# A decoder trunk on one core: GpSimd casts the first weights, x's row blocks are turned in another order, and the low parts of one feed-forward weight tile are taken earlier

## The chip, the cores and the metric

The kernel runs on one core of a Trainium2 chip. The core has five engines that run side by side, each through its own list of instructions in order: TensorE (PE, and PEld for its weight loads) multiplies matrices, VectorE (DVE) and ScalarE (ACT) work element by element and can read the matrix results in PSUM, GpSimd (POOL) works element by element on SBUF, and SyncE (SP) issues most DMAs. An engine waits for another only through semaphores. The metric is the device time in microseconds (us); it is the median of three runs. Before the change it is 1012.55 us (1012.4 to 1013.15).

## What is computed

One layer on 512 rows of width 1024, in float32: a norm, one wide projection, three token mixers, a gated sum, an output projection onto the residual, a second norm, a convolutional feed-forward, and a last norm.

```python
u = rmsnorm(x, ln1_g[i])
proj = u @ w_in[i]
q, k, v, pool_in, z, xbc, dt_raw, gate_pre = jnp.split(proj, split_idx, axis=-1)
...
merged = gates[:, :, 0] * y_a + gates[:, :, 1] * y_b + gates[:, :, 2] * y_c
x = x + merged @ w_o[i]
x = x + conv_ffn(rmsnorm(x, ln2_g[i]), ffn_w_up[i], ffn_conv_w[i], ffn_conv_b[i], ffn_w_down[i])
...
def conv_ffn(u, w_up, conv_w, conv_b, w_down):
    h = causal_dwconv(u @ w_up, conv_w, conv_b)
    a, v = h[..., :D_FF], h[..., D_FF:]
    return (jax.nn.silu(a) * v) @ w_down
```

## The kernel before

Every matrix product is made in three passes. Each operand is split into a high part (a cast to fp32r) and a low part (the value less its high part), and TensorE sums high x high, high x low and low x high (`mm3`, L239). So each weight tile (128 partitions x 2048 elements, mostly) needs, after its DMA, a cast for the high part `wh` (ACT, `cast`, L195) and a subtraction for the low part `wl` (DVE, `low`, L217) before its products can end.

The order of the work on each engine is the order in which the program is written; nothing is rearranged. `trunk` makes a list of jobs, one for each weight tile. In the main loop at the end of it each job, n, is first "prepared": the low part of tile n+1 is taken, the high part of tile n+2 is cast, and the DMA of tile n+3 is issued (`prepare`). Then the job's matmuls are written. A few jobs are marked `late` and call their `prepare` themselves, in two halves: the first `next()` takes the low part of n+1, the second casts n+2 and fetches n+3.

Two places concern the change.

**The start (L1840 to L2000).** The first weight tile comes in two halves of 128 columns (`load_w0`, each 128 x 8 x 128 elements, 512 KB), after the first two row blocks of x. x comes in four row blocks (tb = 0 to 3) of 128 rows, each in two DMAs (`xin`, columns 0 to 511 and 512 to 1023). `turned(tb)` has TensorE transpose the eight 128 x 128 pieces k of a row block into PSUM. Piece k goes to PSUM bank k % 4, where k and k + 4 lie side by side; row block 1 uses three other banks by k % 3. `split_x(tb, k)` then scales each piece by the norm's gain and splits it: ACT writes the high part `xh`, DVE the low part `xl`. Seven matmuls on ones (`warm_up(STILL, 0)`) follow the transposes of row block 1. After that come the products of the first tile with columns 0 to 255 of the rows, by halves j = 0, 1 and by pairs: HH (`h0` x `xh`), HL (`h0` x `xl`), LH (`l0` x `xh`). On TensorE the order is: HH and HL of j = 0, HH of j = 1, the transposes of row block 2, HL of j = 1, LH of j = 0, the transposes of row block 3, LH of j = 1. The high part `h0` of half 0 is cast by DVE (two casts of 128 x 512, L1952), that of half 1 by ACT (L1959); both low parts `l0` are subtracted by POOL (`low0`, L1886).

**The opening of the feed-forward (`up_jobs`, `opening`).** The first two tiles of the up projection start on row blocks 0 and 1 while row blocks 2 and 3 are still being normed. Each of the last two row blocks needs a chain: DVE adds the last product to the residual x (L1376), ACT sums squares (L443), DVE works out the scale (L475 to L478), DVE and ACT scale the two halves of the row block (L482, L483), TensorE transposes them (L457), ACT and DVE split them into `uh` and `ul` (L460, L461). The list `late` holds what is left of the two chains. In half 0 `opening` runs `next(late[1])`, which is the DVE and ACT part of row block 3, then the products of tile 0, then the turn of row block 2, then `next(rest[0])`, the low part of the second up tile. In half 1 it runs two of the three products of tile 1, the turn of row block 3, and the product with that low part.

Of the kernel before, what the change touches and what calls it, by code (L numbers as in the profile page):

```python
# [19 lines left out]
KD = D // P  # L20
# [62 lines left out]
def trunk(ctx: ExitStack, tc, out, x, rel_bias, ln1_g, w_in, b_gate, w_a, pool_w, pool_scale, w_b,  # L83
# [3 lines left out]
    act, dve, pool, pe, sp = nc.scalar, nc.vector, nc.gpsimd, nc.tensor, nc.sync  # L87
# [21 lines left out]
    def MM(name):  # L109
        return psum.tile([P, S], F32, name=name, tag="mm")  # L110

    def SM(name):
        return psum.tile([P, S], F32, name=name, tag="sm")
# [41 lines left out]
    def step():  # L155
        flush()
        if waiting:
            running.append(iter(waiting.pop(0)))
        now = [(it, 0) for it in running]
        for phase in (0, ROWS, WHOLE, REST):  # L160
            now = [(it, advance(it, phase) if at == phase else at) for it, at in now]
# [65 lines left out]
    def wsrc(w, k0, k1, c0, c1):  # L227
        return w[k0 * P:k1 * P, c0:c1].rearrange("(k p) c -> p k c", p=P)
# [14 lines left out]
    def chunk_a(ps, ws, j, xh, xl, ks, lo=0, hi=S, k0=0):  # L243
        wh, wl = ws
        mm3(ps[:, lo:hi], lambda k: wh[:, k0 + k, j * P:(j + 1) * P],
            lambda k: wl[:, k0 + k, j * P:(j + 1) * P],
            lambda k: xh(k)[:, lo:hi], lambda k: xl(k)[:, lo:hi], ks)
# [1204 lines left out]
    def up_evac(m, ps):  # L1452
        t = HC[m] = T("hc")
        act.activation(t, ps, AF.Identity, bias=ff["c1"][:, ff["b"] + m:ff["b"] + m + 1], scale=fw(2, m))  # L1454
        for k in range(2):
            sh = 2 - k
            dve.scalar_tensor_tensor(t[:, sh:], ps[:, :S - sh], fw(k, m), t[:, sh:], OP.mult, OP.add)  # L1457
        if m < KF:
            act.activation(t, t, AF.Silu)  # L1459
            return  # L1460
        a = HC[m - KF]
        pool.tensor_tensor(a, a, t, OP.mult)  # L1462

        def later():
            yield
            k = m - KF
            if k % 2:
                h, l = T("fh", F32R), T("fl", F32R)
                act.copy(h, a)
                it = sums_of(HC[k - 1], a, T("sah", F32R), T("sal", F32R),  # L1470
                             lambda j, h, l: FS.__setitem__((j, k // 2), (h, l)), k >= KS)
                next(it)
                dve.tensor_sub(l, a, h.bitcast(F32))
                ACTS[k] = (h, l)
                yield
                for _ in it:
                    yield
                return
            t = T("f0", F32R)
            act.copy(t[:, :256], a[:, :256])  # L1480
            dve.tensor_sub(t[:, 256:], a[:, :256], t[:, :256].bitcast(F32))
            FS[0, k // 2] = (t[:, :256], t[:, 256:])

        running.append(later())
# [61 lines left out]
    def up_jobs():  # L1546
        held, rest = [], []

        def opening(job, half):
            def body(ws):  # L1550
                uh2, ul2 = nxt["uh"], nxt["ul"]
                if half == 0:
                    rest.append(job.prepare(later=True))
                    next(late[1])
                pss = [MM("pu") for _ in range(2)]

                def product(a, b, i):
                    for j in range(2):
                        for k in range(KD):
                            pe.matmul(pss[j][:, :256], a[:, k, j * P:(j + 1) * P], b[:, k, :256],  # L1560
                                      start=i + k == 0, stop=i == 2 and k == KD - 1)

                product(ws[0], uh2, 0)
                product(ws[0], ul2, 1)
                if half == 0:
                    product(ws[1], uh2, 2)
                next(late.pop(0), None)

                next(rest[0], None)
                if half:  # L1570
                    product(ws[1], uh2, 2)
                for j in range(2):
                    held.append((ws, j, pss[j], KF * half + j))
                if half == 0:
                    return
                for n, (ws_, j, ps, m) in enumerate(held):
                    chunk_a(ps, ws_, j, lambda k: uh2[:, k, :], lambda k: ul2[:, k, :], range(KD), 256, S)
                    if n == 1:
                        job.prepare()
                    up_evac(m, ps)  # L1580
                    step()
            return body

        for p in range(KF // 2):
            for half in range(2):
                def body(ws, p=p, half=half):
                    uh2, ul2 = nxt["uh"], nxt["ul"]
                    for j in range(2):
                        ps = MM("pu")
                        chunk_a(ps, ws, j, lambda k: uh2[:, k, :], lambda k: ul2[:, k, :], range(KD))  # L1590
                        up_evac(KF * half + 2 * p + j, ps)
                        step()
                c = half * DFF + p * 256
                job = Job([wsrc(w_up, 0, KD, c, c + 256)], KD, 256, body)
                if p == 0:
                    job.late = True
                    job.body = opening(job, half)
                yield job
# [258 lines left out]
    raw0 = w0.raw = wraw.tile([P, KD, 256], F32, name="raw", tag="raw")  # L1857
# [19 lines left out]
    h0 = w0.high = whp.tile([P, KD, 256], F32R, name="wh", tag="wh")  # L1877
# [3 lines left out]
    def part(j, k0, k1):  # L1881
        return slice(None), slice(k0, k1), slice(j * P, (j + 1) * P)

    def low0(j, k0, k1):
        o = part(j, k0, k1)
        pool.tensor_tensor(l0[o], raw0[o], h0[o].bitcast(F32), OP.subtract)  # L1886
# [6 lines left out]
    def block(tb, k):  # L1893
        if tb == 1:
            return (uT1, first[2], first[1])[k % 3][:, (k // 3 + 1) * P:(k // 3 + 2) * P]
        return bank(k)[:, tb % 2 * P:tb % 2 * P + P]

    def turned(tb):
        if tb % 2 == 0:
            banks[:] = [SM("uT") for _ in range(4)]  # L1900
        for k in range(KD):
            pe.transpose(block(tb, k), xin[tb, k // 4][:, (k % 4) * P:(k % 4 + 1) * P], eye)

    def split_x(tb, k):
        c = slice(tb * P, (tb + 1) * P)
        act.mul(xh[k][:, c], block(tb, k), g1[:, k:k + 1])
        dve.scalar_tensor_tensor(xl[k][:, c], block(tb, k), g1[:, k:k + 1],
                                 xh[k][:, c].bitcast(F32), OP.mult, OP.subtract)
# [33 lines left out]
    warm_up(WARM)  # L1942
    pe.transpose(first[2][:, :KD], g8[:KD, :P], eye[:KD, :KD])
    turned(0)
    dve.tensor_copy(g1, first[2][:, :KD])
    for k in range(KD):
        split_x(0, k)
    turned(1)
    for k in range(KD):
        if k == 2:  # L1950
            for k0 in (0, 4):
                dve.tensor_copy(h0[part(0, k0, k0 + 4)], raw0[part(0, k0, k0 + 4)])  # L1952
            low0(0, 0, KD)
        split_x(1, k)
    warm_up(STILL, 0)
    group(0, (HH,), 0, 256)
# [6 lines left out]
    half_squares(dve, 0, 1)  # L1963
    group(1, (HH,), 0, 256)
    turned(2)
    for k in range(KD):
        split_x(2, k)
# [112 lines left out]
```

## Time and profile before

| | |
|---|---|
| median of three runs | 1012.55 us (1012.4 to 1013.15) |
| the profiled execution | 1012.54 us, of which 1010.8 us from the first instruction to the last |
| PE busy | 999.7 us, 99% of the span |
| DVE, ACT, POOL busy | 753.7, 534.7, 137.8 us |
| DMA | 127.03 MB, 126 GB/s |

A row of the timeline reads: start, time from the first to the last of the merged instructions, engine, line, operation, output <- inputs, shapes, count, and in brackets the idle time of the engine before it with what ended that. All times are us from the start of the span. SPq and ACTq are DMAs being issued by SP and ACT; a DMA lands later.

### The profile page before, as it was taken

How to read it: one execution, taken by the hardware profiler on the slowest of the kernel's cores; microseconds unless marked ns; L12 is line 12 of the kernel's file. 1: busy time of each engine (PE TensorE's matmuls, PEld its weight loads, DVE VectorE, ACT ScalarE, POOL GpSimd, SP SyncE). 2: the span in 40 equal slices, each digit the busy share in tenths (PEclk: the TensorE clock that was granted, in tenths of full speed). 3: DMA queues.
4: the chain of work that ended last, by engine and by line, in shares of the span. 5: the costliest groups of instructions: out<-in, count | busy, mean ns of one | idle time of the engine just before them, and what ended most of it. 6: DMA issues, size and time to landing. Idle time of an engine off the chain costs nothing.

```text
span 1010.8 us, 13607 instructions
## 1 busy us (share of the span) xinstructions
PE 999.7 (99%) x5307; PEld 850.0 (84%) x5307; DVE 753.7 (75%) x962; ACT 534.7 (53%) x929; POOL 137.8 (14%) x111
## 2 busy tenths in 40 slices
PE   9999999999999999999999999999999999999996
PEld 8898878999988888888888888898888888888885
DVE  6995668677767645776889888868778768685877
ACT  6343546554445566888566246554444434443456
POOL 4400010110000000000044501302111100121032
PEclk9999999999999999999999999999999999999999
DMA  7344360755343435552254754232352134542573
GB/s 221 102 126 131 106 187 4 193 150 147 102 155 94 108 100 132 146 137 62 77 152 125 211 188 90 80 126 84 99 193 84 50 117 149 175 115 73 146 184 109
DMA packets 117735, 127.03 MB, mean 126 GB/s; under 512 B 6791, under 2 KB 96462, under 8 KB 117671
## 3 DMA queue, kind: packets, MB, share of 16 engines
q1 hardware_dynamic: 112327, 116.98, 37.4%
q0 software_dynamic: 5040, 8.65, 5.4%
q8 instruction: 42, 0.69, 0.3%
q10 hardware_dynamic: 304, 0.53, 0.1%
q14 instruction: 22, 0.18, 0.1%
HBM read 121.56 MB, written 3.00 MB: 123 GB/s over the span
## 4 chain that ended last, share of the span: by engine, by line
PE 96%; DVE 2%; ACT 0%; DMA 0%; issue 0%; ACTq 0%
PE pa L239 37%; PE pu L239 23%; PE pb L239 10%; PE pd L239 8%; PE pqk L239 6%; PE pq L239 3%; PE ps L810 1%; PE pa L1918 1%; PE ppw L239 1%; PE po L858 1%; PE pt L844 1%; PE py L1140 1%; DVE wl L217 1%; PE pyo L1147 1%; PE pst L1128 0%; DMA xin<-in_x_dram 0%
## 5 line engine op out<-in xcount | busy, mean ns | idle before, releaser
L217 DVE TENSOR_TENSOR wl<-raw,wh 128x2048 fp32r<-128x2048 f32 (+3 forms) x86 | 205.9, 2396 | 32.9 <-ACT wh L195 24.2
L195 ACT CAST wh<-raw 128x1024 fp32r<-128x1024 f32 (+2 forms) x168 | 167.0, 1011 | 53.0 <-DVE raw L362 17.8
L1457 DVE SCALAR_TENSOR_TENSOR hc<-pu,fcol,hc 128x510 f32<-128x510 f32 x88 | 65.9, 748 | 53.7 <-ACT hc L1454 52.0
L239 PE MATMUL pu<-uh,wh 128*128 128x512 f32 (+1 forms) x352 | 83.6, 379 | 0.0
L239 PE MATMUL pu<-uh,wl 128*128 128x512 f32 (+1 forms) x352 | 83.5, 379 | 0.0
L239 PE MATMUL pu<-ul,wh 128*128 128x512 f32 (+1 forms) x352 | 83.5, 379 | 0.0
L239 PE MATMUL pa<-uh,wh 128*128 128x512 f32 (+1 forms) x336 | 80.9, 380 | 0.0
L239 PE MATMUL pa<-ul,wh 128*128 128x512 f32 (+1 forms) x336 | 78.9, 374 | 0.0
L239 PE MATMUL pa<-uh,wl 128*128 128x512 f32 (+1 forms) x336 | 78.8, 374 | 0.0
L239 PEld LDWEIGHTS pu<-ul,wh 128*128 128x128 f32 x352 | 64.2, 188 | 12.5
L239 PEld LDWEIGHTS pu<-uh,wl 128*128 128x128 f32 x352 | 64.2, 188 | 12.4
L239 PEld LDWEIGHTS pu<-uh,wh 128*128 128x128 f32 x352 | 64.1, 188 | 12.4
L1454 ACT ACTIVATE hc<-pu,fcol,fcol 128x512 f32<-128x512 f32 x40 | 31.2, 779 | 75.7 <-PE pu L239 75.7
L239 PEld LDWEIGHTS pa<-ul,wh 128*128 128x128 f32 x336 | 60.7, 188 | 11.4
L239 PEld LDWEIGHTS pa<-uh,wl 128*128 128x128 f32 x336 | 60.7, 188 | 11.2
L239 PEld LDWEIGHTS pa<-uh,wh 128*128 128x128 f32 x336 | 59.4, 189 | 10.6
L1462 POOL TENSOR_TENSOR hc<-hc 128x512 f32<-128x512 f32 x22 | 29.9, 1360 | 279.0 <-DVE hc L1457 243.3
L217 DVE TENSOR_TENSOR wl<-w,wh 128x2048 fp32r<-128x2048 f32 (+1 forms) x26 | 54.3, 2088 | 9.8 <-issue 4.5
L195 ACT CAST wh<-w 128x1024 fp32r<-128x1024 f32 (+1 forms) x52 | 47.2, 950 | 8.6 <-DMA w<-in_ffn_w_down_dram 3.8
L832 ACT ACTIVATE sb<-sb,nmls 128x128 f32<-128x128 f32 (+1 forms) x72 | 30.0, 418 | 32.5 <-DVE nmls L829 21.9
L1459 ACT ACTIVATE hc<-hc 128x512 f32<-128x512 f32 x22 | 13.9, 633 | 40.3 <-DVE hc L1457 40.3
L1123 POOL TENSOR_TENSOR st<-st,dts 128x512 f32<-128x512 f32 x4 | 4.2, 1051 | 225.4 <-ACT st L1131 164.9
(461 smaller groups left out, 2012.8 us busy)
## 6 DMA issues: line engine op xcount, KB each, us to landing
raw<-in_w_in_dram SPq DMA_DIRECT2D x24, 1024.0 KB, 5.5
raw<-in_ffn_w_up_dram SPq DMA_DIRECT2D x22, 1024.0 KB, 5.1
raw<-in_w_in_dram SPq DMA_DIRECT2D x14, 512.0 KB, 4.0
raw<-in_w_in_dram SPq DMA_DIRECT2D x8, 768.0 KB
raw<-in_ffn_w_down_dram SPq DMA_DIRECT2D x6, 1024.0 KB, 4.9
raw<-in_w_b_dram SPq DMA_DIRECT2D x4, 1024.0 KB
al<-ad SPq DMA_DIRECT2D x16, 256.0 KB, 7.9
raw<-in_w_c_dram SPq DMA_DIRECT2D x4, 1024.0 KB, 5.3
```

Source lines behind the costliest of these rows:

```text
L195: (other.tensor_copy if other and i else act.copy)(job.high[:, :, o], job.raw[:, :, o])
L217: (eng or dve).tensor_tensor(l[:, :, o], job.raw[:, :, o], h[:, :, o].bitcast(F32), OP.subtract)
L239: pe.matmul(ps, l, r, start=first and n == 0, stop=last and n == total - 1, skip_group_check=onto)
L810: pe.matmul(pss[i][:, o:o + w * P], q[r, n * P:(n + 1) * P], k[r, kb * P:(kb + w) * P], start=True, stop=True)
L832: act.activation(sb[:, off:off + w * P], sb[:, off:off + w * P], AF.Exp, bias=nm[:, n, h:h + 1], accum_out=ls[:, n, h:h + 1])
L844: pe.transpose(pt[:, o:o + P], sb[:, o:o + P], eye)
L858: pe.matmul(po[DH * hh:DH * hh + DH, n * P:(n + 1) * P], V[g, kb + i][:, (2 * c + hh) * DH:(2 * c + hh + 1) * DH], probs[2 * c + hh, nb][: ...
L1140: pe.matmul(py[DH * i:DH * i + DH, j * P:(j + 1) * P], xc[:, o:o + DH], als[j // 2][:, lo:lo + P], start=True, stop=True)
L1454: act.activation(t, ps, AF.Identity, bias=ff["c1"][:, ff["b"] + m:ff["b"] + m + 1], scale=fw(2, m))
L1457: dve.scalar_tensor_tensor(t[:, sh:], ps[:, :S - sh], fw(k, m), t[:, sh:], OP.mult, OP.add)
L1459: act.activation(t, t, AF.Silu)
L1462: pool.tensor_tensor(a, a, t, OP.mult)
```

## The change

At the start, POOL instead of DVE casts half 0 of the first weight tile, ahead of POOL's own subtractions and with no DVE work in between; the casts no longer stand between DVE's splits of row block 1. The transposes of every row block are written in the order 0, 4, 1, 5, 2, 6, 3, 7, so that the two pieces of one bank follow each other; the splits keep the order 0 to 7. In the opening of the feed-forward, the low part of the second up tile is written ahead of row block 3's chain instead of behind row block 2's turn; the second half of that `prepare` (cast and fetch) stays in half 1.

```diff
@@ opening
                 if half == 0:
                     rest.append(job.prepare(later=True))
+                    next(rest[0])
                     next(late[1])
...
                 next(late.pop(0), None)
 
-                next(rest[0], None)
                 if half:
+                    next(rest[0], None)
                     product(ws[1], uh2, 2)
@@ turned
-        for k in range(KD):
+        for k in (0, 4, 1, 5, 2, 6, 3, 7):
             pe.transpose(block(tb, k), xin[tb, k // 4][:, (k % 4) * P:(k % 4 + 1) * P], eye)
@@ the start
     turned(1)
+    for k0 in (0, 4):
+        pool.tensor_copy(h0[part(0, k0, k0 + 4)], raw0[part(0, k0, k0 + 4)])
+    low0(0, 0, KD)
     for k in range(KD):
-        if k == 2:
-            for k0 in (0, 4):
-                dve.tensor_copy(h0[part(0, k0, k0 + 4)], raw0[part(0, k0, k0 + 4)])
-            low0(0, 0, KD)
         split_x(1, k)
```

On POOL, at the start of the program, this is the difference. The CAST rows are the casts of `h0`, the TENSOR_TENSOR rows of `wl` are the two subtractions. The row ISA is not written in the kernel: the build puts it there, and it is the instruction that has a library of GpSimd routines loaded. The build places one such instruction ahead of the first POOL instruction whose routine is in a library; a subtraction's is, a cast's is not.

```order
 L2062 MEMSET const-uint8-127 128x1
 L2076 UNCONDITIONAL_BRANCH
-L1886 ISA
-L1886 TENSOR_TENSOR wl<-raw,wh 128x8x128 x2
+L1951 CAST wh<-raw 128x4x128 x2
+L1887 ISA
+L1887 TENSOR_TENSOR wl<-raw,wh 128x8x128 x2
 L1973 TENSOR_TENSOR xf<-xh,xl 128x256 x8
 L642 TENSOR_TENSOR xf<-xf,rows 128x512 x8
```

Before, the ISA instruction was the first thing on POOL's list; now it stands behind two casts that need the weights from memory, and ahead of the first subtraction.

On DVE, in the opening of the feed-forward, these rows stood before. The `va`, `vo`, `v`, `r`, `rt`, `u` rows are row block 3's chain, the `ul` rows are the splits of row blocks 2 and 3, and the L217 row is the low part of the second up tile.

```order
L1376 TENSOR_TENSOR x_5515<-x_5515,pb 128x512
L1330 TENSOR_SCALAR va_106<-so_105 128x1
L1331 TENSOR_SCALAR vo_107<-va_106 128x1
L475 SCALAR_TENSOR_TENSOR v<-ss,vo_107 128x1
L476 RECIPROCAL r<-sq 128x1
L477 SCALAR_TENSOR_TENSOR rt<-r,v 128x1
L478 SCALAR_TENSOR_TENSOR rt<-rt,r 128x1
L482 SCALAR_TENSOR_TENSOR u_5961<-x_5515,rt,grow 128x512
L461 TENSOR_TENSOR ul_5789<-uT,uh_5788 128x4x128 x2
L217 TENSOR_TENSOR wl<-raw,wh 128x2048
L461 TENSOR_TENSOR ul_5789<-uT,uh_5788 128x4x128 x2
```

And these now, in the same place:

```order
L1376 TENSOR_TENSOR x_5515<-x_5515,pb 128x512
L1330 TENSOR_SCALAR va_106<-so_105 128x1
L1331 TENSOR_SCALAR vo_107<-va_106 128x1
L217 TENSOR_TENSOR wl<-raw,wh 128x2048
L475 SCALAR_TENSOR_TENSOR v<-ss,vo_107 128x1
L476 RECIPROCAL r<-sq 128x1
L477 SCALAR_TENSOR_TENSOR rt<-r,v 128x1
L478 SCALAR_TENSOR_TENSOR rt<-rt,r 128x1
L482 SCALAR_TENSOR_TENSOR u_5961<-x_5515,rt,grow 128x512
L461 TENSOR_TENSOR ul_5789<-uT,uh_5788 128x4x128 x4
```

The low part moved up by seven instructions, ahead of the scale of row block 3, and both row blocks' `ul` now follow each other.

## The prediction

> **What bounds the kernel now.** I read the page first, then the list of what TensorE waited for, then the timeline of the two places that the change touches.
>
> ```profile
> span 1010.8 us, 13607 instructions
> ...
> PE 999.7 (99%) x5307; PEld 850.0 (84%) x5307; DVE 753.7 (75%) x962; ACT 534.7 (53%) x929; POOL 137.8 (14%) x111
> ...
> PE 96%; DVE 2%; ACT 0%; DMA 0%; issue 0%; ACTq 0%
> ```
>
> ```profile
> PE pa L1854 <- DVE ones L1843: 1.1, 1, 1.1
> PE pa L1918 <- ACT xh L1906: 0.8, 1, 0.8
> PE pu L1560 <- DVE wl L217: 0.6, 1, 0.6
> PE uT L1902 <- DMA xin<-in_x_dram: 0.5, 1, 0.5
> ```
>
> TensorE is busy for 99% of the span, and the chain that ended last lies on it for 96%. The second fence is its whole list of waits: 3.0 us in four places. So nothing on the other engines can win more than a few us, but whatever makes TensorE wait anywhere is added in full, since nothing behind it has slack to give back. The change touches the second wait (the start) and the third (the opening of the feed-forward). The profiled execution took 1012.54 us, the median of the three runs is 1012.55 us, so sums against the one hold for the other.
>
> **The start, as it is.** These are rows of the timeline of the first 20 us.
>
> ```profile
> 1.06 3.85 PE L1854 MATMUL pa<-ones 128*128 128x128 f32 x20 [1.06 <-DVE ones L1843]
> ...
> 1.76 1.28 ACT L1847 ACT_TABLE_LOAD   x1 [1.76 <-issue]
> 2.60 1.06 SPq L1860 DMA_DIRECT2D raw<-in_w_in_dram  x2
> ...
> 5.61 1.20 PE L1902 MATMUL uT<-eye,xin 128*128 128x128 f32 x9 [0.55 <-DMA xin<-in_x_dram]
> 6.41 2.43 ACT L1906 ACTIVATE xh<-uT,g 128x128 fp32r<-128x128 f32 x9 [3.16 <-PE uT L1902]
> ...
> 7.41 1.73 PE L1854 MATMUL pa<-ones 128*128 128x128 f32 x14
> ...
> 9.41 0.76 DVE L1952 CAST wh<-raw 128x512 fp32r<-128x512 f32 x2
> ...
> 9.97 1.81 PE L1918 MATMUL pa<-xh,wh 128*128 128x256 f32 x8 [0.83 <-ACT xh L1906]
> ...
> 10.24 5.20 POOL L1886 TENSOR_TENSOR wl<-raw,wh 128x1024 fp32r<-128x1024 f32 x2 [9.80 <-DVE wh L1952]
> ...
> 10.46 0.37 ACT L1906 ACTIVATE xh<-pa,g 128x128 fp32r<-128x128 f32 x1 [0.56 <-DVE xl L1907]
> ...
> 11.62 1.10 PE L1918 MATMUL pa<-xl,wh 128*128 128x256 f32 x8
> ...
> 14.31 1.20 PE L1918 MATMUL pa<-xl,wh 128*128 128x256 f32 x8
> ...
> 15.34 1.12 PE L1918 MATMUL pa<-xh,wl 128*128 128x256 f32 x8
> ...
> 17.04 0.40 SPq L182 DMA_DIRECT2D raw<-in_w_in_dram  x1
> ...
> 17.41 1.20 PE L1918 MATMUL pa<-xh,wl 128*128 128x256 f32 x8
> ```
>
> The rows at 15.34 and 17.41 are the ones that decide: they are the LH products of halves 0 and 1, and they need POOL's two subtractions, which run from 10.24 to 15.44. Before, the first was done 2.7 us ahead of its product and the second 2.0 us ahead. The time from issue to landing of the two weight halves, and the costs of POOL's instructions by shape, are in these rows.
>
> ```profile
> raw<-in_w_in_dram SPq DMA_DIRECT2D x2, 512.0 KB, 6.0
> ```
>
> ```profile
> L908 POOL TENSOR_TENSOR o<-o,wb 128x512 f32<-128x512 f32 x9 | 16.3, 1840 | 8.1 <-DMA wb<-wd 8.1
> ...
> L1321 POOL TENSOR_TENSOR xg<-x,grow 128x512 f32<-128x512 f32 x4 | 9.2, 2299 | 16.7 <-DVE x L1376 16.7
> ...
> L1886 POOL TENSOR_TENSOR wl<-raw,wh 128x1024 fp32r<-128x1024 f32 x2 | 5.2, 2626 | 9.8 <-DVE wh L1952 9.8
> L1123 POOL TENSOR_TENSOR st<-st,dts 128x512 f32<-128x512 f32 x4 | 4.2, 1051 | 225.4 <-ACT st L1131 164.9
> ```
>
> **The casts on POOL.** Half 0 lands at about 2.60 + 6.0 = 8.6, so POOL can cast from 8.6 where DVE began at 9.41. No row shows a cast on POOL. From below, DVE does one in 0.42 (two in 0.76); from above, a POOL operation of the same 128x512 takes 2.30 with two inputs (L1321). The quick POOL row (1.05) has long idle time ahead of it, the slower ones come in crowded stretches, and from 8 to 12 us DVE is busy throughout:
>
> ```profile
> 2.00:4.00 2.00, 2.00 (x12) 2.00 (x11) 0.00 (x0) 1.25 (x2) 0.00 (x0) 1.00 0.80 170
> ...
> 8.00:9.00 1.00, 1.00 (x11) 0.95 (x9) 1.00 (x5) 1.00 (x6) 0.00 (x0) 1.00 1.21 292
> ...
> 11.00:12.00 1.00, 1.00 (x7) 0.85 (x8) 1.00 (x4) 1.00 (x4) 1.00 (x1) 1.00 1.05 384
> ```
>
> (columns: window, its length, busy time of PE, PEld, DVE, ACT, POOL, then granted clock, DMA share, GB/s). So I take 1.8 each, by L908, and the second ends at 8.6 + 3.6 = 12.2. By the Trainium skill, GPSIMD Engine Reference, section Elementwise, a good one-input loop over 512 elements takes 769 ns; two of them would be an estimated 1.5 us in place of 3.6 and the sum 2.1 us less. No run here shows which.
>
> **The library.** This is the step on which I rest the forecast. Before, the ISA instruction stood first on POOL's list, in 9.80 us in which POOL did nothing else (L1886). Whatever it costs was hidden there. Now POOL reaches it after the casts, at 12.2, with the subtractions queued right behind it and TensorE waiting for those. Its cost has no row. From below it is 0, since an idle engine shows nothing; from above 9.8, the idle time in which it had to be over. The nearest rows are a load of the same kind on another engine (ACT_TABLE_LOAD, 1.28) and a fetch from memory in this stretch (6.0 to landing, with the DMA engines full, share 1.05 to 1.21). Code has to be fetched and then taken in, so I add the two: 7.3. The Trainium skill, GPSIMD Engine Reference, section Instruction dispatch, speaks against the change: the first call to freshly loaded code pays about 6 us (5.95), with no instruction in the profile for it. By that figure the sum would be 1.3 us less; the idle time before agrees in that it would have hidden it.
>
> **What that does to TensorE.** The first subtraction starts at 8.6 + 3.6 + 7.3 = 19.5 and takes 2.4 (half of 5.20, less for the first), so LH of half 0 starts at 22.0 in place of 15.34: 6.7 later. The second subtraction ends at about 24.7; LH of half 1 would follow at 24.7 in place of 17.41, 7.3 later. Meanwhile TensorE has run out: with the second cast at 12.2 its HL starts at 12.7 in place of 11.62, so the HL product of half 1 (14.31, about 1.0 long) ends near 16.4, and it idles 5.6 us. After its idle time at the start it ran 20 records in 3.85 us, later 14 in 1.73, at which pace 20 take 2.5: 1.4 us lost to a slow array, though the granted clock of 2 to 4 us reads 1.00. The same after 5.6 us of idle puts LH of half 1 at 22.0 + 2.07 + 1.4 = 25.5, 8.1 later, which is past the 7.3. I take 8.0. The bounds: casts of 2.3 and a load of 9.8 give 8.6 + 4.6 + 9.8 + 2.4 = 25.4, hence 10.1 + 1.4 = 11.5; casts of 0.42 with no load leave the subtractions early.
>
> Late next are POOL's eight `xf` additions behind the subtractions and, on SP, the fetch of the third weight tile, which needs the raw buffer that the second subtraction reads. Before, that fetch was issued at 17.04 and its tile was wanted by TensorE at 35.4:
>
> ```profile
> 24.47 10.92 PE pa L239 x48
> 35.46 21.82 PE pa L239 x96
> ```
>
> Its 18 us shrink to about 43.4 - 24.7 = 18.7, so nothing more is lost.
>
> **DVE freed, and the order of the transposes.** ACT started its splits at 6.41, when the fifth transpose (the second of bank 0) was through; with pieces 0 and 4 first it can start after two, three steps of 0.11 earlier, 0.33. Without the two casts DVE saves 0.67 and ACT's 0.56 of waiting goes. So the first HL could come 1.0 earlier, and row blocks 2 and 3 might save 0.3. But the product behind them needs POOL's casts too, and those now end last, so here I count 0; these gains stand only in the rivals. A transpose of row block 1 asks for its second DMA 0.33 earlier; before it did not wait, and ACT needs that row block only 1 us later, so 0 too.
>
> **The opening of the feed-forward.**
>
> ```profile
> 660.13 0.15 DVE L1330 TENSOR_SCALAR va<-so 128x1 f32<-128x1 f32 x1
> ...
> 660.43 1.03 PE L457 MATMUL uT<-eye,u 128*128 128x128 f32 x8
> ...
> 661.22 2.15 PE L1560 MATMUL pu<-uh,wh 128*128 128x256 f32 x16
> ...
> 661.98 0.75 DVE L482 SCALAR_TENSOR_TENSOR u<-x,rt,grow 128x512 f32<-128x512 f32 x1
> 662.03 0.72 ACT L483 ACTIVATE u<-xg,rt 128x512 f32<-128x512 f32 x1 [0.74 <-DVE rt L478]
> ...
> 664.47 2.28 DVE L217 TENSOR_TENSOR wl<-raw,wh 128x2048 fp32r<-128x2048 f32 x1
> ...
> 665.13 1.04 PE L457 MATMUL uT<-eye,u 128*128 128x128 f32 x8
> ...
> 666.80 1.46 PE L1560 MATMUL pu<-uh,wl 128*128 128x256 f32 x10 [0.64 <-DVE wl L217]
> ```
>
> Eight transposes hold TensorE 0.79 (660.43 to 661.22); after those at 665.13 the next product could start at 665.92 but starts at 666.80, when the low part is done. Moved to 660.4, it ends at 662.7. Row block 3's `u` follows about 0.8 of scale work later, at 663.5 to 664.3, and its transposes at 665.13 still have 0.8 to spare. On ACT the `uh` of row block 2 goes behind that and ends by 665.4, before row block 3's at 665.76. So 0.9 is won (0.64 by the bracket).
>
> **The sum.** 1012.54 + 8.0 - 0.9 = 1019.6 us.
>
> **Rivals.** One, the other side: the ISA instruction costs nothing (the same library may be there already) and POOL casts at DVE's pace. Then both casts end by 9.4, TensorE gains the 1.0 and 0.3 at the start, and the time is 1012.54 - 0.9 - 1.3 = 1010.3. It decides where the two casts end before about 9.9 and casts plus load stay under 3.3 us (14.3 - 8.6 - 2.4). For it speaks that the first subtraction began 0.07 after DVE's cast, with no start-up cost of its own; against it, that the idle time would have swallowed any. Two: no load, but casts of 1.8. The products start 1.1 later, 0.2 comes back in the transposes, and with 0.9 won later the time is 1012.5, no change. A short load belongs here too: casts and load together of 5.2 us give exactly nothing (15.34 + 0.9 - 8.6 - 2.4). Three: the forecast's mechanism with the low ends, casts of 1.05 and a load of 6.0: 8.6 + 2.1 + 6.0 + 2.4 = 19.1, 3.8 later, 1.4 for the slow array, so 1016.8.
>
> **The numbers.** 0.2% is 2.0 us, about what a measurement of this kernel tells from no change. Chances: the load on the path, at any size from 7.2 us of casts and load upwards, 0.81 (slower); rival two, 0.12 (same); rival one, 0.07 (faster). The range takes in the forecast's mechanism from the 0.2% border, 1014.5, to its upper bound, 1012.54 + 11.5 - 0.9 = 1023; the other two cases, 0.19, stay outside.
>
> **What would show it.** In the timeline of the first 30 us: the L1886 subtraction starting near 19.5 with idle time ahead of it that no engine's work explains, then TensorE's wait for POOL's `wl` at the LH product, several us long, at the head of its list of waits; POOL's cast rows show 1.8 or something else. In the opening, TensorE's 0.6 wait for `wl` gone. If TensorE has no wait for POOL beyond 1 us, the library costs nothing and I am wrong in the main step; if the wait is there but under 3 us, the load is mis-sized.

## The result, and the profile after

The changed kernel takes 1010.59 us (1010.12 to 1011.15), against 1012.68 us (1011.96 to 1013.46) for the kernel before, measured beside it: a ratio of 0.9979, 95% interval 0.9972 to 0.9985. It is faster by 2.1 us, where I forecast 1019.6 us. The profiled execution took 1010.22 us, 2.3 us less than that of before, so the two traces can be laid side by side. These are the span, the busy times and the chain that ended last on the page of the changed kernel:

```profile
span 1008.5 us, 13607 instructions
...
PE 999.1 (99%) x5307; PEld 849.9 (84%) x5307; DVE 752.5 (75%) x960; ACT 534.8 (53%) x929; POOL 137.6 (14%) x113
...
PE 98%; DMA 1%; DVE 0%; SPq 0%; POOL 0%; issue 0%
```

DVE has two instructions less and POOL two more, as the change says. The start of the chain has another course. Before, it went over the fetch of x, then over DVE's splits and casts (DVE held 2%):

```profile
1.36 4.20 DMA xin<-in_x_dram
...
6.81 2.68 DVE xl L1907 x10
9.49 0.67 DVE wh L1952 x2
```

Now it goes over the fetch of the weights' half 0 and POOL's first cast, and no longer over DVE:

```profile
2.60 6.03 DMA raw<-in_w_in_dram
...
8.68 0.62 POOL wh L1951
```

TensorE's whole list of waits (total, times, longest, in us) has shrunk from four to two:

```profile
PE pa L1855 <- DVE ones L1844: 1.1, 1, 1.1
PE pa L1919 <- POOL wh L1951: 0.2, 1, 0.2
```

The wait of 0.8 for ACT's `xh` at the start and the wait of 0.6 for `wl` in the opening are gone. In place of the first stands 0.2 for POOL's cast. The fourth wait, 0.5 for x's DMA, is gone too, but not by the change: it is also missing in the kernel that has only the change in the opening, whose start is as before. The wait of several us for POOL's `wl`, on which my forecast rested, is not there. The timeline of the start, with the instructions that answer to those shown of before (line numbers have moved by one):

```profile
5.31 1.20 PE L1903 MATMUL uT<-eye,xin 128*128 128x128 f32 x9
...
5.79 2.43 ACT L1907 ACTIVATE xh<-uT,g 128x128 fp32r<-128x128 f32 x9 [2.53 <-PE uT L1903]
...
8.68 1.17 POOL L1951 CAST wh<-raw 128x512 fp32r<-128x512 f32 x2 [8.24 <-DMA raw<-in_w_in_dram]
...
9.35 1.30 PE L1919 MATMUL pa<-xh,wh 128*128 128x256 f32 x8 [0.17 <-POOL wh L1951]
...
9.93 5.22 POOL L1887 TENSOR_TENSOR wl<-raw,wh 128x1024 fp32r<-128x1024 f32 x2
...
10.48 1.12 PE L1919 MATMUL pa<-xl,wh 128*128 128x256 f32 x8
...
14.23 1.12 PE L1919 MATMUL pa<-xh,wl 128*128 128x256 f32 x8
...
15.18 1.04 PE L1903 MATMUL uT<-eye,xin 128*128 128x128 f32 x8
...
15.97 1.20 PE L1919 MATMUL pa<-xh,wl 128*128 128x256 f32 x8
```

The two casts take 1.17 us together, from 8.68 to 9.85. The first subtraction follows at 9.93, 0.08 us behind them; the row carries no bracket, so POOL had no idle time to speak of. Whatever the library instruction costs, it is inside those 0.08 us. So the LH products start at 14.23 and 15.97, where they started at 15.34 and 17.41: 1.11 and 1.44 us earlier. The view of the subtractions' line shows the library instruction itself:

```profile
L1887 POOLq MODIFY_POOL_CONFIG  x2: 11/11/11, 9.8 to 9.8; - x2
L1887 POOL TENSOR_TENSOR wl<-raw,wh x2: 2410/2634/2858, 9.9 to 12.3; 128x1024 fp32r<-128x1024 f32 x2
```

(columns: shortest, median and longest duration in ns, then first and last start in us.) It is the pair MODIFY_POOL_CONFIG, of 11 ns each, at 9.8 us, on POOL's queue. In the kernel before, the same pair stood near the head of the 9.80 us of idle time:

```profile
L1886 POOLq MODIFY_POOL_CONFIG  x2: 11/11/11, 0.7 to 0.8; - x2
```

In the opening of the feed-forward the timeline of the changed kernel reads:

```profile
658.91 2.28 DVE L217 TENSOR_TENSOR wl<-raw,wh 128x2048 fp32r<-128x2048 f32 x1
...
661.82 0.75 DVE L482 SCALAR_TENSOR_TENSOR u<-x,rt,grow 128x512 f32<-128x512 f32 x1
661.88 0.73 ACT L483 ACTIVATE u<-xg,rt 128x512 f32<-128x512 f32 x1 [2.05 <-DVE rt L478]
...
663.64 1.04 PE L457 MATMUL uT<-eye,u 128*128 128x128 f32 x8
...
664.43 2.15 PE L1561 MATMUL pu<-uh,wl 128*128 128x256 f32 x16
```

The product with the low part follows the transposes by 0.79 us (663.64 to 664.43), where it followed by 1.67 before. Row block 3's scale comes later on DVE, ACT waits 2.05 us for it, and the transposes still start without a wait. Counted from the same product before, the gain is 1.44 us at the second LH product and 2.37 us behind the opening (666.80 to 664.43): 1.44 at the start, 0.9 in the opening, and nothing given back.

### The profile page after: what moved, and what is told of

Same layout as the page of the kernel before. It is cut to its first block, busy times and chain, and to the rows that moved or that the text cites. A ratio compares the mean times of both kernels' runs of the same rounds, so it can differ in the third digit from the quotient of the medians.

```text
span 1008.5 us, 13607 instructions
## 1 busy us (share of the span) xinstructions
PE 999.1 (99%) x5307; PEld 849.9 (84%) x5307; DVE 752.5 (75%) x960; ACT 534.8 (53%) x929; POOL 137.6 (14%) x113
## 4 chain that ended last, share of the span: by engine, by line
PE 98%; DMA 1%; DVE 0%; SPq 0%; POOL 0%; issue 0%
PE pa L239 37%; PE pu L239 23%; PE pb L239 11%; PE pd L239 8%; PE pqk L239 6%; PE pq L239 3%; PE ps L810 1%; PE pa L1919 1%; PE pu L1561 1%; PE ppw L239 1%; PE po L858 1%; PE pt L844 1%; PE py L1140 1%; DMA raw<-in_w_in_dram 1%; PE pyo L1147 1%; PE pst L1128 0%
## 5 line engine op out<-in xcount | busy, mean ns | idle before, releaser
L217 DVE TENSOR_TENSOR wl<-raw,wh 128x2048 fp32r<-128x2048 f32 (+3 forms) x86 | 203.6, 2369 | 34.5 <-ACT wh L195 26.1
L217 DVE TENSOR_TENSOR wl<-w,wh 128x2048 fp32r<-128x2048 f32 (+1 forms) x26 | 54.2, 2086 | 10.2 <-issue 4.5
```

The costliest lines, as they stand in the source:

```text
L217: (eng or dve).tensor_tensor(l[:, :, o], job.raw[:, :, o], h[:, :, o].bitcast(F32), OP.subtract)
```

## The experiments

### The opening alone

The kernel before, with only the low part of the second up tile ahead of row block 3's chain.

```diff
                 if half == 0:
                     rest.append(job.prepare(later=True))
+                    next(rest[0])
                     next(late[1])
...
                 next(late.pop(0), None)
-                next(rest[0], None)
                 if half:
+                    next(rest[0], None)
                     product(ws[1], uh2, 2)
```

> Only the opening of the feed-forward is changed; the start stays as before. Theory (the three parts add up, and this one takes away the wait for the low part): TensorE's 0.6 us wait for wl goes, the products after row block 3's transposes start 0.79 us after them instead of 1.67, and the time is 0.9 us less than before, about 1011.8. Rival (the start's gain uncovered most of it, or the moved chain costs as much elsewhere): within 0.3 us of before.

Measured: 1011.66 us against 1012.68, ratio 0.9992 (0.9984 to 1.0001), so about -1.0 us. TensorE's list of waits in this kernel:

```profile
PE pa L1855 <- DVE ones L1844: 1.1, 1, 1.1
PE pa L1919 <- ACT xh L1907: 0.8, 1, 0.8
```

The wait for `wl` is gone and the one at the start stands as before. The size is as worked out. The interval just touches 1, so from these times alone it is likely rather than shown; the vanished wait is what shows the mechanism. A second comparison agrees: the changed kernel without the opening, further down, is 0.8 us slower than the changed kernel beside it (1011.64 against 1010.82).

### The casts alone

The kernel before, with only the casts moved to POOL.

```diff
+    for k0 in (0, 4):
+        pool.tensor_copy(h0[part(0, k0, k0 + 4)], raw0[part(0, k0, k0 + 4)])
+    low0(0, 0, KD)
     for k in range(KD):
-        if k == 2:
-            for k0 in (0, 4):
-                dve.tensor_copy(h0[part(0, k0, k0 + 4)], raw0[part(0, k0, k0 + 4)])
-            low0(0, 0, KD)
         split_x(1, k)
```

> Only the casts go to GpSimd; the transposes keep the order 0 to 7 and the opening stays as before. Theory (DVE's queue was the hold-up): the casts take 0.6 us each from 8.7, the first HL product starts 1.0 us earlier than before's 11.62, and the time is 0.9 to 1.1 us less than before. Rival (the order of the transposes does most of it): 0.3 us less or nothing.

Measured: 1012.27 us against 1012.68, ratio 0.9995 (0.9986 to 1.0004): -0.4 us, less than expected and not told from no change. Its timeline shows that the library instruction is free here too (the casts end at 9.93, the subtraction starts at 10.01), and that the first product waits for the cast:

```profile
8.77 1.16 POOL L1950 CAST wh<-raw 128x512 fp32r<-128x512 f32 x2 [8.32 <-DMA raw<-in_w_in_dram]
...
10.01 5.21 POOL L1886 TENSOR_TENSOR wl<-raw,wh 128x1024 fp32r<-128x1024 f32 x2
```

```profile
9.43 1.50 PE L1918 MATMUL pa<-xh,wh 128*128 128x256 f32 x8 [0.47 <-POOL wh L1950]
```

### The order of the transposes alone

The kernel before, with only the new order of the pieces.

```diff
-        for k in range(KD):
+        for k in (0, 4, 1, 5, 2, 6, 3, 7):
```

> Only the order of the transposes is changed; DVE still casts between its splits. Theory: ACT starts its splits 0.3 us earlier and everything behind follows, and the transposes of row blocks 2 and 3 save another 0.2 to 0.3; 0.3 to 0.6 us less than before. Rival (the DVE casts hold the splits, so nothing gets through): within 0.2 us of before.

Measured: 1011.95 us against 1012.68, ratio 0.9994 (0.9986 to 1.0003): -0.7 us, a little more than expected, and by itself not told from no change. TensorE's wait for ACT's `xh` at the first product went from 0.8 to 0.5:

```profile
PE pa L1918 <- ACT xh L1906: 0.5, 1, 0.5
```

One part of its gain can be read inside each trace. The transposes of row block 3 hold TensorE 1.11 us before (from 16.30 to the next product at 17.41) and 0.79 here (16.57 to 17.36):

```profile
16.30 1.35 PE L1902 MATMUL uT<-eye,xin 128*128 128x128 f32 x8
```

```profile
16.57 1.04 PE L1902 MATMUL uT<-eye,xin 128*128 128x128 f32 x8
```

(the first row is of the kernel before, the second of this one.) The other two kernels with the old order need 1.10 as well, and the kernels with the new order 0.79, but for the one with another library, whose array ran slowly there. So 0.3 of the gain at the start is the order's.

### The casts and the order, without the opening

The changed kernel, with the move in the opening undone (the diff of the first experiment, reversed).

> The casts on GpSimd and the order of the transposes together, without the move in the opening of the feed-forward. Theory (the parts add up, and of the start the two belong together): 1.2 us under before, 0.9 over the changed kernel, about 1011.5. Rival (the start's gain is no more than that of the two parts alone at their lowest): 0.5 us or less under before.

Measured: 1011.64 us against 1012.64, ratio 0.9990 (0.9981 to 0.9998): -1.0 us. The wait for `wl` in the opening is back:

```profile
PE pu L1560 <- DVE wl L217: 0.7, 1, 0.7
```

So the change consists of -1.0 at the start and -1.0 in the opening, which make its -2.1. Within the start, -0.4 for the casts and -0.7 for the order make -1.1. Apart from the 0.3 in the transposes of row block 3, how the start divides between the two is known no better than the intervals of some 0.9 us to either side allow.

### Another library ahead of the casts

This is the run that tests the main step of my forecast. The theory after the result: the library instruction is free because the library that it names is already in GpSimd. The rival: it is free in any case, and GpSimd loads nothing that matters. The changed kernel gets one POOL instruction of a different library early on, whose output nobody reads. The build puts a library instruction ahead of it (L1849), and the one ahead of the subtractions stays where it was in the changed kernel.

```diff
+    pool.partition_broadcast(cpool.tile([P, 1], F32, name="spread"), eps[:1, :])
```

> The changed kernel with one small GpSimd instruction of another library (a broadcast of one element) ahead of the casts, in idle time. The library instruction ahead of the first subtraction stays where it is, but the library that it names is no longer the one that is loaded. Theory (the instruction was free because its library was loaded already): now it costs several us between the casts (end near 9.9) and the first subtraction; with 6 to 7 us the LH product starts at 18.5 to 19.5 instead of 14.23, and the time is 4 to 7 us over the changed kernel's, 1015 to 1018. Rival (the instruction never holds GpSimd up, whatever is loaded): the subtraction starts near 9.9 and the time is within 0.3 us of the changed kernel's.

Measured: 1019.7 us (1018.63 to 1020.31) against 1012.68, ratio 1.0067 (1.0054 to 1.0080), 9.1 us more than the changed kernel and above the 4 to 7 that I expected. POOL's timeline of the first 30 us:

```profile
8.16 0.28 POOL L1849 PARTITION_BROADCAST spread<-eps  x1 [7.72 <-DVE xl L1909]
8.95 1.17 POOL L1952 CAST wh<-raw 128x512 fp32r<-128x512 f32 x2 [0.51 <-DMA raw<-in_w_in_dram]
18.39 4.66 POOL L1888 TENSOR_TENSOR wl<-raw,wh 128x1024 fp32r<-128x1024 f32 x2 [8.27 <-issue]
```

The casts are over at 10.12 and the first subtraction starts at 18.39: 8.27 us of idle time, put down to "issue", that is, to nothing that the profile shows. The broadcast was done before the weights had landed and so delayed no cast itself. Its own 7.72 us of idle time, put down to a split of DVE that it doesn't use, is likely the change to its library. Its pair of library instructions stood at 1.0 us, so 7.1 us bounds that change from above:

```profile
L1849 POOLq MODIFY_POOL_CONFIG  x2: 11/11/11, 1.0 to 1.0; - x2
```

The line of the subtractions shows the same two instructions of about 11 ns as in the changed kernel, at 10.1 us:

```profile
L1888 POOLq MODIFY_POOL_CONFIG  x2: 13/13/13, 10.1 to 10.2; - x2
```

TensorE's list of waits and its timeline:

```profile
PE pa L1920 <- POOL wl L1888: 5.5, 1, 5.5
```

```profile
14.11 1.20 PE L1920 MATMUL pa<-xl,wh 128*128 128x256 f32 x8
20.78 2.08 PE L1920 MATMUL pa<-xh,wl 128*128 128x256 f32 x8 [5.47 <-POOL wl L1888]
22.65 1.82 PE L1904 MATMUL uT<-eye,xin 128*128 128x128 f32 x8
24.21 1.21 PE L1920 MATMUL pa<-xh,wl 128*128 128x256 f32 x8
```

The first LH product starts 6.55 us later than in the changed kernel (20.78 against 14.23), the second 8.24 later (24.21 against 15.97). The other 1.7 us are the slow array: the same eight matmuls take 2.08 instead of 1.12, the transposes 1.82 instead of 1.04. Here the granted clock shows it (columns as in the prediction):

```profile
18.00:20.00 2.00, 0.00 (x0) 0.00 (x0) 0.00 (x0) 0.00 (x0) 1.61 (x1) 0.50 0.03 9
20.00:22.00 2.00, 1.22 (x5) 1.22 (x6) 0.00 (x0) 0.00 (x0) 2.00 (x2) 0.50 0.00 0
22.00:24.00 2.00, 2.00 (x12) 2.00 (x11) 0.28 (x1) 0.62 (x2) 2.00 (x3) 0.50 0.00 0
24.00:26.00 2.00, 2.00 (x18) 2.00 (x17) 1.85 (x8) 1.94 (x8) 2.00 (x4) 0.94 0.82 222
```

The rival falls: changing the library costs 8.3 us, as an instruction of 13 ns followed by a gap that names no one. What the instruction costs depends on what is loaded when it is reached. When the library of the subtractions came to be there in the changed kernel (by default, or left by the execution before) was not tried and stays open.

### Each cast twice

The changed kernel, with each of POOL's two casts written twice, so that what they cost is seen by itself.

```diff
     for k0 in (0, 4):
-        pool.tensor_copy(h0[part(0, k0, k0 + 4)], raw0[part(0, k0, k0 + 4)])
+        for _ in range(2):
+            pool.tensor_copy(h0[part(0, k0, k0 + 4)], raw0[part(0, k0, k0 + 4)])
```

> The changed kernel with each of the two GpSimd casts written twice, about 2.3 us of casts instead of 1.2 (the output is the same). Theory (casts of 1.2 each would have put the start back on GpSimd): the second cast ends at about 11.0, the first HL product starts 1.0 to 1.1 us later than 10.48, and the time is 1.0 us over the changed kernel's. Rival (the casts are covered): within 0.3 us of it.

Measured: 1011.83 us against 1012.64, ratio 0.9991 (0.9983 to 1.0000), 1.0 us more than the changed kernel in the same comparison (1010.82). POOL's casts, and what TensorE waited for:

```profile
8.41 3.06 POOL L1952 CAST wh<-raw 128x512 fp32r<-128x512 f32 x4 [7.97 <-DMA raw<-in_w_in_dram]
```

```profile
PE pa L1919 <- POOL wh L1952: 1.6, 2, 1.0
```

POOL needs 1.9 us more (3.06 against 1.17), and by the medians 1.0 of that reaches the end. So the casts are on the path of the first products. Casts of 1.8 us each, 2.4 more in all than measured, would by this proportion have cost some 1.3 us (2.4 x 1.0 / 1.9), more than the whole gain of the start: an estimate from this pair.

### Four smaller casts

The changed kernel, with four casts of 128x256 in place of two of 128x512, so that the first product could start on less.

```diff
-    for k0 in (0, 4):
-        pool.tensor_copy(h0[part(0, k0, k0 + 4)], raw0[part(0, k0, k0 + 4)])
+    for k0 in (0, 2, 4, 6):
+        pool.tensor_copy(h0[part(0, k0, k0 + 2)], raw0[part(0, k0, k0 + 2)])
```

> The changed kernel with four GpSimd casts of 128x256 instead of two of 128x512, so that TensorE can begin after the first quarter. Theory (the start now hangs on the landing of the first weights at 8.6 and the length of the first cast): the first product starts 0.3 us earlier, at about 9.0, the first HL product at about 10.2 instead of 10.48, and the time is 0.3 us under the changed kernel's, about 1010.3. Rival (the splits of x or the fixed cost of two more casts take it back): no change.

Measured: 1010.98 us against 1012.64, ratio 0.9982 (0.9974 to 0.9991), no better than the changed kernel beside it. A miss. The casts cost 1.43 us instead of 1.17, and in this execution the first product did not hang on them:

```profile
5.83 1.89 PE L1903 MATMUL uT<-eye,xin 128*128 128x128 f32 x9
...
9.80 1.79 PE L1919 MATMUL pa<-xh,wh 128*128 128x256 f32 x8
```

The transposes of row block 0 and the first of row block 1 still ran slowly (1.89 against 1.20 in the changed kernel), and the product follows seven matmuls on ones without a wait.

### The changed kernel once more

No edit. It shows how far the start of one kernel varies.

> The changed kernel once more, beside the others of this batch: 1010.6 by every theory. Its profile shows how far the start differs from one execution to another: by the theory that the array's slow time at the start ends at another moment in each execution, the twenty records of the first warm-up take between 3.9 and 4.6 us, and the first product still starts within 0.1 us of 9.35, since it hangs on the weights and not on the transposes.

Measured: 1010.82 us against 1012.64, ratio 0.9982 (0.9973 to 0.9991). The time repeats; the start in its trace does not:

```profile
7.59 0.63 PE L1903 MATMUL pa<-eye,xin 128*128 128x128 f32 x4 [0.82 <-DVE xl L1908]
...
9.33 1.17 POOL L1951 CAST wh<-raw 128x512 fp32r<-128x512 f32 x2 [8.89 <-DMA raw<-in_w_in_dram]
...
10.00 1.30 PE L1919 MATMUL pa<-xh,wh 128*128 128x256 f32 x8
```

The weights landed 0.65 us later than in the other execution (the casts start at 9.33 against 8.68), TensorE waited 0.82 us ahead of row block 1's transposes, and the first product started at 10.00 against 9.35, outside what I had expected. Its row carries no bracket, so this trace doesn't tell which of the two held it. So differences of a few tenths between two traces of the start say nothing; I compare stretches within one trace, or medians.

## Why the prediction was wrong, point by point

- **The library: wrong, and it decides.** The step put 7.3 us of loading between the casts and the first subtraction. In the changed kernel that gap is 0.08 us. The step took "the idle time before would have hidden it" as leave to take a value from rows of another kind. The low end, 0, which I had as a bound, was the true one. What followed from the step was right: with a library that does have to be loaded, the gap is 8.27 (7.3 in the step), TensorE waits 5.47 (5.6), the slow array costs 1.7 (1.4), the LH products start at 20.78 and 24.21 (22.0 and 25.5), and the time is 1019.7 (1019.6). That the two times agree so closely is partly luck: the forecast's casts were 2.4 us too long and its load 1.0 too short, and the profiled execution of that kernel took 1018.76. The mechanism was sound; its condition, that the library is not there, did not hold. The Trainium skill, GPSIMD Engine Reference, section Instruction dispatch, states the 5.95 us for freshly loaded code; the changed kernel pays nothing of the sort (0.08), and the kernel with another library, where the instruction names what is not loaded, shows 8.27.
- **The casts on POOL: the size was off by three.** I took 1.8 us each from POOL operations with two inputs; they take 0.61, nearer to DVE's 0.42. The Trainium skill, GPSIMD Engine Reference, section Elementwise, gives 769 ns as the best case for 512 elements, which was closer than my row and still above the measurement.
- **DVE freed and the order of the transposes: the sizes were about right, the 0 was wrong.** I worked out 1.0 and 0.3 and counted neither, since the product behind was to wait for POOL. In the trace HL of half 0 starts 1.14 us earlier (11.62 to 10.48), and the second LH product another 0.3 (1.44 in all). The 0.3 comes back in every trace with the new order but the slow one of the kernel with another library. The 1.14 is one pair of executions: with the start unchanged, in the kernel with the opening alone, HL starts at 12.29 instead of 11.62. The medians say -1.0 for the two together.
- **The opening: right.** -0.9 was forecast; the spacing behind the transposes is 0.79 as worked out, and the opening alone measured -1.0. Row block 3's chain had the slack that the step gave it.
- **What would be late next: nothing was.** TensorE's only new wait is 0.2 us. The transposes of row block 1, which now ask for their second DMA earlier, did wait in some executions: 0.2 us, put down to the DMA of x, with each cast written twice, and 0.8 in the repeat of the changed kernel, put down there to DVE's `xl`, which a transpose doesn't read; that it was the same DMA is likely and not shown. On SP, the 18 us ahead of the third weight tile do not shrink in the prediction's own figures, as it says: they come to 18.7. Nothing hangs on it.
- **The rival that held.** Rival one gave 1010.3 us; 1010.59 was measured. It asked for casts that end before about 9.9, and they end at 9.85, though at 0.61 each and not at DVE's pace. I gave it 0.07. The row that spoke for it, the subtraction that began 0.07 us behind DVE's cast, was the same in both worlds, so it should have left the two nearer to even.

## What to carry to other kernels

An idle engine hides a cost that may be zero: idle time ahead of an instruction bounds a cost from above only, and a price from another engine does not make it likely. On GpSimd, moving work ahead of the first instruction of a library was free here; mixing instructions of two libraries cost 8.3 us at the switch, and as much as was not covered reached the end. One-input work on GpSimd should not be priced by its two-input rows: the cast took 0.61 us at a shape where two-input rows took 1.05 to 2.30.

## What the runs showed of the hardware that I had not expected

**The library switch is nearly invisible.** It is a pair of instructions of 11 to 13 ns, listed under the line of the next instruction, then a gap of 8.27 us put down to "issue". The same pair in the changed kernel is followed at once.

**The slow array at the start isn't in the granted clock, the later one is.** During the 5.47 us of waiting the clock column fell to 0.50, and it came back to 0.94 in the stretch from 24 to 26 us. At the very start, where the warm-up's matmuls run just as slowly, the column reads 1.00. The Trainium skill, TensorE: Matmul & The Clock Gate, Part 1, says that an idle window of about 3.4 us halves the clock. The trace of the kernel with another library shows the half, but less idle time ahead of it: the last product before the wait ends at 15.31 (14.11 + 1.20), and the clock falls in this stretch, some 2.1 us later (the column reads 1.00 just before it and 0.50 just behind):

```profile
17.40:17.50 0.10, 0.00 (x0) 0.00 (x0) 0.00 (x0) 0.00 (x0) 0.00 (x0) 0.65 1.21 143
```

The Trainium skill also says, in the same part, that the moment of the change of pace at the start varies, since the window runs freely. The runs agree in that the same 20 warm-up matmuls took from 3.85 us in the kernel before to 4.64 in others, with the code ahead of them unchanged, and 4.17 and 4.32 in two executions of the changed kernel:

```profile
1.06 4.64 PE L1854 MATMUL pa<-ones 128*128 128x128 f32 x20 [1.06 <-DVE ones L1843]
```

(timeline of the kernel with the casts and the order, without the opening.)
